# Up projection: the transfers that put aside the sums of pairs, begun by ScalarE in place of GpSimd

## The chip, the cores and the metric

The kernel runs on one core of one Trainium2 chip. The time is the device time of one execution in microseconds (us). A core has five engines that each work through their own list of instructions in order: TensorE (PE, with its weight loads, PEld), VectorE (DVE), ScalarE (ACT), GpSimd (POOL) and SyncE (SP). Transfers between the chip's DRAM and the on-chip SBUF are begun by an instruction on one of these lists (here on SP's, POOL's or ACT's) and are then carried by 16 DMA engines; an instruction that needs their data waits on a semaphore that the transfer raises when it has landed.

## The reference

One layer of a diffusion backbone: 512 latent tokens and 256 context tokens of width 2048, all in float32. A modulated RMS norm, one input projection, attention beside a gated short convolution, an output projection, then the gated MLP that this change concerns, and a final norm. The MLP, cut to what matters:

```
def dwconv3(x, w, b):
    xp = jnp.pad(x, ((0, 0), (1, 1), (0, 0)))
    return xp[:, :-2] * w[0] + xp[:, 1:-1] * w[1] + xp[:, 2:] * w[2] + b

def conv_ffn(h, w_up, cw, cb, w_down):          # FFN_DIM = 5504 = 43 tiles of 128
    u = dwconv3(h @ w_up, cw, cb)
    a, g = jnp.split(u, 2, axis=-1)
    return (a * jax.nn.silu(g)) @ w_down
```

## The kernel before

Activations lie transposed: features on the 128 partitions, the 512 tokens along a row, in two halves of 256 (H0, H1). Float32 operands are split in a high part that the TensorE takes as it is (a cast on ACT, line 1023 for weights) and a low part (the difference, on DVE, line 1024).

**Up projection.** A loop over `f` runs through 43 tiles of the hidden width; a step makes one tile of the gate (`cg`) and one of the value (`ca`). From `f` = 3 on, a step is a two-by-two block product in seven products instead of eight (weights `a11`, `a12`, `a22` and the sums `s1`, `s3`; operands of the tokens prepared once, the tiles `hf` and `T`). In the trace the products of step 12 are called u12p1, u12p2, u12p6, u12q5, u12p7, u12q4 and u12q3. p1, p6, p7 and q4 add up in one bank of PSUM, `u12a`; between them ACT must copy the partial sum out (`aside`, line 1224) before PE may go on adding to that bank. Steps overlap: q4 and q3 of a step run among p1, p2 and p6 of the next. The high and low parts of the weights live in three buffers each (`wh`, `wl`), so ACT can cast at most a product or so ahead of PE.

**Weights.** `up_load` (lines 1141 to 1152) has SP load five tiles of 512 KB per step; to two of them (`s1`, `s3`) a second block of weights is added by an accumulating transfer that POOL begins (line 1151, in the trace `u_s<-in_w_up`), as soon as the first has landed.

**Sums of pairs.** The down projection after it is a block product of the same kind, so it needs seven sums of each pair of activation tiles. `pair_sums` makes them while the up projection runs, for 18 pairs (steps 7 and 8, 9 and 10, and so on): `put` (lines 1065 to 1076) takes a source of 256 tokens, casts its high part into a tile `tp` on ACT (line 1074), has DVE write the low part behind it (line 1075), and begins a transfer of the tile, 256 KB, to the DRAM tensor `t_d` (line 1076). There are 126 of them, named in the program after the pair and the sum, `tp13` for sum "3" of pair 1. `pair_sums` is a generator that is advanced by one sum after every second product. The `tp` tiles come from pools with hardly a spare buffer at this time: the tile of sum "21" takes the place of the tile of sum "3" of the same pair, so its cast (line 1074) can't start before the transfer of sum "3" has landed.

**What sets the order.** The program is written in one order, and a scheduler with a simulated clock then decides how the instructions stand on each engine; only a few are tied (`tc.issue_after` puts the cast of a `put` behind the last cast of weights). An engine takes its list strictly in order. A transfer begun by SP or by ACT raises one of eight semaphores, which both use in turn; those begun by POOL have eight of their own. Where a semaphore is used again, its last transfer must have landed before the next is begun.

Of the kernel before, what the change touches and what calls it, by code (L numbers as in the profile page):

```python
# [10 lines left out]
F32 = mybir.dt.float32  # L11
# [61 lines left out]
def block_kernel(ctx, tc, xt, ctxt, ctxn, c, c_ctx, w_ada, small, w_in, w_inc, w_q, w_kv, w_out,  # L73
# [3 lines left out]
    V, A, G_, PE, SP = nc.vector, nc.scalar, nc.gpsimd, nc.tensor, nc.sync  # L77
# [15 lines left out]
    t_d = dr.tile([PAIRS, 7, P, T], F32, name="t_d")  # L93
# [3 lines left out]
    def t2(shape, dt, name):  # L97
        return act.tile(shape, dt, tag="t2", bufs=NT2, name=name)

    def tmp(shape, dt, name):  # L100
        return tp.tile(shape, dt, tag="tmp", bufs=5, name=name)
# [956 lines left out]
    OPS = ("11", "21", "2", "1", "3", "4", "22")  # L1058

    def pair_sums(p, e, o):  # L1060


        t = tmp([P, T], F32, f"ts{p}") if p == PAIRS - 1 else cp.tile([P, T], F32, tag="ts", bufs=1, name=f"ts{p}")

        def put(n, src):

            nth["tp"] += 1
            if nth["tp"] % 3 or p == PAIRS - 1:
                z = t2([P, T], F32R, f"tp{p}{n}")
            else:  # L1070
                z = cp.tile([P, T], F32R, tag="tq", bufs=1, name=f"tp{p}{n}")

            with tc.issue_after(last_hi[0]):
                A.copy(out=z[:, :256], in_=src)  # L1074
            V.tensor_tensor(out=z[:, 256:], in0=src, in1=z[:, :256].bitcast(F32), op=ALU.subtract)  # L1075
            G_.dma_start(t_d[p, OPS.index(n)], z.bitcast(F32))  # L1076

        put("11", e[:, H0])
        yield
        V.tensor_tensor(out=t[:, H0], in0=e[:, H0], in1=e[:, H1], op=ALU.subtract)  # L1080
        put("1", t[:, H0])
        yield
        V.tensor_tensor(out=e[:, H1], in0=o[:, H1], in1=e[:, H1], op=ALU.subtract)
        put("3", e[:, H1])
        yield
        put("22", o[:, H1])
        yield
        V.scalar_tensor_tensor(out=t[:, H1], in0=t[:, H0], scalar=-1.0, in1=o[:, H1], op0=ALU.mult, op1=ALU.subtract)
        put("2", t[:, H1])
        yield  # L1090
        put("21", o[:, H0])
        yield
        V.scalar_tensor_tensor(out=o[:, H0], in0=t[:, H1], scalar=-1.0, in1=o[:, H0], op0=ALU.mult, op1=ALU.subtract)
        put("4", o[:, H0])
        yield
# [378 lines left out]
    for st in range(STEPS - 2):  # L1474
        z = nxt
# [172 lines left out]
```

## Time and profile before

| | |
|---|---|
| median of 3 runs | 2161.89 us (2161.41, 2161.89, 2166.99) |
| profiled execution | 2159.29 us, of it 2157.2 us between its first and last instruction (the span) |
| PE busy in the span | 2095.5 us, 97% |
| DVE, ACT, POOL busy | 1825.5, 1046.5 and 187.9 us |
| mean granted TensorE clock | 0.991 of full speed |
| steps of the up projection by block products | from about 880 us to 1693 us |
| casts of `put` (line 1074), first and last | 1001.1 and 1739.8 us |

"Busy" counts the time in which an engine executes; beginning a transfer is not counted on SP and ACT. Where a row gives idle time and a releaser (`<-`), the engine stood that long before the instruction, and the releaser is what came last. An engine's idle time costs something only where PE then stands too. TensorE's clock is granted in stretches, and a row of a time window shows the mean clock in it (1.00 is full speed).

### The profile page before, as it was taken

The numbers are of one execution on the slowest core, as the hardware profiler recorded it, in microseconds if no ns is written. First come the engines' busy times: TensorE is split into PE (matmuls) and PEld (weight loads), VectorE is DVE, ScalarE is ACT, GpSimd is POOL, SyncE is SP. The second block draws the span as 40 slices with busy tenths as digits, with TensorE's granted clock in tenths as the row PEclk, the third lists the DMA queues.
The fourth block names the chain that finished last, engine by engine and source line by source line (L and its number), as shares of the span: only waits on it lengthen the run. The fifth ranks groups of instructions, "written<-read, shape, count | busy, mean of one in ns | idle before, by whom it ended". The sixth has DMA issues, their size and how long they took to land.

```text
span 2157.2 us, 35425 instructions
## 1 busy us (share of the span) xinstructions
PE 2095.5 (97%) x13268; PEld 1883.6 (87%) x13268; DVE 1825.5 (85%) x3024; ACT 1046.5 (49%) x1715; POOL 187.9 (9%) x270
## 2 busy tenths in 40 slices
PE   7899999999999999999999999999999999999997
PEld 4688788888888889999899898989989889999997
DVE  7998987778886989898889898888989748888887
ACT  5533333555553237555556555555555433333445
POOL 0000000000000000111111111211111100000000
PEclk9999999999999999999999999999999999999998
DMA  9989885334559985687778777778778999878683
GB/s 336 337 279 342 269 281 178 129 125 158 181 199 349 364 277 178 166 221 205 224 210 233 219 230 226 212 227 229 221 224 235 345 311 303 258 235 243 201 252 113
DMA packets 162112, 513.75 MB, mean 238 GB/s; under 512 B 18962, under 2 KB 23314, under 8 KB 156306
## 3 DMA queue, kind: packets, MB, share of 16 engines
q1 hardware_dynamic: 133364, 418.14, 56.7%
q0 software_dynamic: 27488, 92.29, 18.1%
q8 instruction: 104, 1.70, 0.3%
q10 hardware_dynamic: 1088, 1.05, 0.1%
q14 instruction: 68, 0.56, 0.1%
HBM read 464.22 MB, written 46.14 MB: 237 GB/s over the span
## 4 chain that ended last, share of the span: by engine, by line
PE 78%; DMA 11%; DVE 7%; issue 2%; ACT 2%; POOL 0%; DVEq 0%; SPq 0%; POOLq 0%; ACTq 0%
DMA t_d<-tp 4%; PE pp L187 4%; PE pp L189 4%; PE pp L188 3%; DMA u_s<-in_w_up 3%; DMA ada<-in_w_ada 2%; PE o L189 1%; PE o L187 1%; PE o L188 1%; PE d L187 1%; PE d L189 1%; PE d L188 1%; PE uf L187 1%; PE uf L188 1%; PE uf L189 1%
## 5 line engine op out<-in xcount | busy, mean ns | idle before, releaser
L1076 POOL DMA_DIRECT2D t_d<-tp x126 | 81.1, 657 | 442.5 <-DVE tp L1075 431.5
L1151 POOL DMA_DIRECT2D u_s<-in_w_up x80 | 70.1, 877 | 274.4 <-DMA u_s<-in_w_up 204.0
L263 DVE SCALAR_TENSOR_TENSOR ada<-ada,sv 128x1024 f32<-128x1024 f32 x68 | 82.3, 1223 | 12.4 <-DMA ada<-in_w_ada 12.4
L166 ACT CAST w_0h<-rw 128x512 fp32r<-128x512 f32 (+1 forms) x63 | 38.3, 618 | 105.9 <-PE pp L188 59.4
L241 DVE SCALAR_TENSOR_TENSOR ada<-ada,sv 128x1024 f32<-128x1024 f32 x64 | 78.2, 1230 | 5.8 <-DMA ada<-in_w_ada 5.6
L530 DVE SCALAR_TENSOR_TENSOR ada<-ada,svc 128x1024 f32<-128x1024 f32 x64 | 75.9, 1222 | 2.0 <-DMA ada<-in_w_ada 2.0
L1074 ACT CAST tp<-a 128x256 fp32r<-128x256 f32 x90 | 35.9, 406 | 67.6 <-DMA t_d<-tp 53.2
L793 POOL TENSOR_TENSOR gr<-gr,half 128x8 f32<-128x8 f32 x4 | 10.1, 2523 | 628.1 <-DVE gr L792 536.2
L167 DVE TENSOR_TENSOR w_0l<-rw,w_0h 128x512 fp32r<-128x512 f32 (+1 forms) x63 | 43.1, 691 | 22.1 <-ACT w_0h L166 21.8
L1075 DVE TENSOR_TENSOR tp<-a,tp 128x256 fp32r<-128x256 f32 x90 | 38.0, 423 | 24.6 <-ACT tp L1074 24.6
L263 DVE SCALAR_TENSOR_TENSOR ra<-ra,sv 128x1024 f32<-128x1024 f32 x44 | 52.5, 1220 | 1.1 <-DMA ra<-in_w_ada 1.0
L1265 DVE TENSOR_TENSOR u<-u,u_s 128x1024 f32<-128x1024 f32 x40 | 48.9, 1221 | 5.2 <-DMA u_s<-in_w_up 5.0
L1266 DVE TENSOR_TENSOR u<-u,u 128x1024 f32<-128x1024 f32 x40 | 48.8, 1220 | 0.0
L764 ACT CAST pth<-t 128x384 fp32r<-128x384 f32 x64 | 28.6, 485 | 26.7 <-PE t L761 26.7
L541 DVE TENSOR_TENSOR acc<-acc,pp 128x512 f32<-128x512 f32 x50 | 34.7, 693 | 2.1 <-PE pp L189 2.1
L765 DVE TENSOR_TENSOR ptl<-t,pth 128x384 fp32r<-128x384 f32 x64 | 33.3, 552 | 2.7 <-ACT pth L764 2.7
L745 DVE TENSOR_REDUCE mn<-s 128x1 f32<-128x768 f32 x32 | 30.4, 954 | 5.1 <-PE s L734 4.9
L1038 ACT ACTIVATE g<-g 128x512 f32<-128x512 f32 x43 | 27.2, 632 | 15.2 <-DVE g L1032 14.8
L1030 ACT ACTIVATE g<-cg,sm 128x512 f32<-128x512 f32 x40 | 32.6, 815 | 0.0
L1030 ACT ACTIVATE a<-ca,sm 128x512 f32<-128x512 f32 x40 | 32.1, 802 | 0.0
L748 ACT ACTIVATE p<-s,mn 128x768 f32<-128x768 f32 x32 | 29.3, 915 | 1.6 <-DVE mn L745 1.3
L1032 DVE SCALAR_TENSOR_TENSOR a<-ca,sm,a 128x511 f32<-128x511 f32 x40 | 29.9, 747 | 0.0
(10239 smaller groups left out, 8970.6 us busy)
## 6 DMA issues: line engine op xcount, KB each, us to landing
ada<-in_w_ada SPq DMA_DIRECT2D x196, 512.0 KB, 5.9
u<-in_w_up SPq DMA_DIRECT2D x120, 512.0 KB, 8.9
w<-t_d SPq DMA_DIRECT2D x161, 256.0 KB, 5.0
u_s<-in_w_up SPq DMA_DIRECT2D x80, 512.0 KB, 4.0
u_s<-in_w_up POOLq DMA_DIRECT2D x80, 512.0 KB, 9.7
t_d<-tp POOLq DMA_DIRECT2D x126, 256.0 KB, 8.6
v<-in_w_dnw SPq DMA_DIRECT2D x72, 384.0 KB, 5.1
ra<-in_w_ada SPq DMA_DIRECT2D x22, 1024.0 KB, 4.7
```

Source lines behind the costliest of these rows:

```text
L167: V.tensor_tensor(out=lo[:, :n], in0=raw[:, a:a + n], in1=hi[:, :n].bitcast(F32), op=ALU.subtract)
L187: PE.matmul(ps, w[0], x[0], start=first, stop=False, skip_group_check=on_top)
L188: PE.matmul(ps, w[0], x[1], start=False, stop=False, skip_group_check=on_top)
L189: PE.matmul(ps, w[1], x[0], start=False, stop=last, skip_group_check=on_top)
L241: V.scalar_tensor_tensor(out=r, in0=r, scalar=1.0, in1=vec[:, i * 1024:(i + 1) * 1024], op0=ALU.mult, op1=ALU.mult, accum_out=col[:, i:i + 1])
L263: keep(V.scalar_tensor_tensor(out=r, in0=r, scalar=1.0, in1=svs[i], op0=ALU.mult, op1=ALU.mult, accum_out=lc[:, t % 4:t % 4 + 1] if i else ...
L530: keep(V.scalar_tensor_tensor(out=raw[q], in0=raw[q], scalar=1.0, in1=svc[:, q * 1024:(q + 1) * 1024], op0=ALU.mult, op1=ALU.mult, accum_o ...
L1030: A.activation(u, src, AF.Identity, bias=s("fb", m), scale=s("fw", 86 + m))
L1076: G_.dma_start(t_d[p, OPS.index(n)], z.bitcast(F32))
L1151: G_.dma_start(r[-1], src[more], accum_op=ALU.add)
L1265: V.tensor_tensor(out=a11, in0=a11, in1=s1, op=ALU.add)
L1266: V.tensor_tensor(out=a12, in0=a12, in1=a11, op=ALU.add)
```

## The change

One word: the transfer at the end of `put` is begun on ACT's list instead of POOL's. Each of the 126 transfers waits, as before, for DVE's part of the tile (line 1075).

```
             with tc.issue_after(last_hi[0]):
                 A.copy(out=z[:, :256], in_=src)
             V.tensor_tensor(out=z[:, 256:], in0=src, in1=z[:, :256].bitcast(F32), op=ALU.subtract)
-            G_.dma_start(t_d[p, OPS.index(n)], z.bitcast(F32))
+            A.dma_start(t_d[p, OPS.index(n)], z.bitcast(F32))
```

The scheduler then moves instructions on other engines too, each by a few places. Three places matter below. A minus marks a row that stood there before, a plus a row that stands there now; the number behind a name counts tiles through the program.

POOL's list around steps 10 to 12 (`u_s` are the weights `s1` and `s3`):

```order
 L1151 DMA u_s_9774<-in_w_up 128x1024
 L1151 DMA u_s_9777<-in_w_up 128x1024
-L1076 DMA t_d<-tp_9923 128x512
-L1076 DMA t_d<-tp_9978 128x512
-L1076 DMA t_d<-tp_10104 128x512
 L1151 DMA u_s_9991<-in_w_up 128x1024
-L1076 DMA t_d<-tp_10054 128x512
 L1151 DMA u_s_9994<-in_w_up 128x1024
```

Only the accumulating transfers stay on POOL's list in this part of the program.

ACT's list in step 12, where `tp_10501` is sum "3" and `tp_10551` sum "22" of pair 1:

```order
 L1074 CAST tp_10551<-a_10336 128x256
 L1023 CAST u12p6h<-u_11_10208 128x1024
+L1076 DMA t_d<-tp_10501 128x512
+L1076 DMA t_d<-tp_10551 128x512
+L1230 ACTIVATE ca_10431<-u11a 128x256
 L1023 CAST u12q5h<-u_s_10212 128x1024
 L1074 CAST tp_10618<-ts_10369 128x256
-L1230 ACTIVATE ca_10431<-u11a 128x256
```

The two transfers stand behind the cast for product p6 and ahead of that for q5. In other pairs (step 14, for example) sum "22" comes first and sum "3" second at the same place.

ACT's list in step 14, where `tp_11146` is sum "21" of pair 2 and `u_11042` the copy of bank `u14a` that product p7 waits for:

```order
 L1023 CAST u15p1h<-u_11_10881 128x1024
+L1074 CAST tp_11146<-a_10783 128x256
 L1224 COPY u_11042<-u14a 128x256
-L1074 CAST tp_11146<-a_10783 128x256
 L1038 ACTIVATE g_11004<-g_11004 128x512
 L1023 CAST u15p2h<-u_12_10883 128x1024
+L1076 DMA t_d<-tp_11146 128x512
 L1023 CAST u14q4h<-u_22_10665 128x1024
```

The cast of sum "21" now stands ahead of the copy. Before, it stood ahead of it in six steps (10, 12, 18, 24, 30 and 36) and behind it in ten (14, 16, 20, 22, 26, 28, 32, 34, 38 and 40); now it stands ahead of it in all sixteen.

On PE's list the first matrix product of q4 (or of p2, or of q3) is placed a few rows earlier in some steps, and on SP's list a few loads after the up projection change places.

More of the change, by code (lines that the diff above doesn't have):

```diff
@@ L1075, in put @@
             V.tensor_tensor(out=z[:, 256:], in0=src, in1=z[:, :256].bitcast(F32), op=ALU.subtract)
-            G_.dma_start(t_d[p, OPS.index(n)], z.bitcast(F32))
+            A.dma_start(t_d[p, OPS.index(n)], z.bitcast(F32))
         put("11", e[:, H0])
```

## The prediction

> **What bounds the kernel now.** I read the groups of instructions first, because the change touches three of them: the transfers of `put`, the accumulating transfers beside them, and the casts that start each `put`.
>
> ```profile
> L1076 POOL DMA_DIRECT2D t_d<-tp x126 | 81.1, 657 | 442.5 <-DVE tp L1075 431.5
> L1151 POOL DMA_DIRECT2D u_s<-in_w_up x80 | 70.1, 877 | 274.4 <-DMA u_s<-in_w_up 204.0
> L1074 ACT CAST tp<-a 128x256 fp32r<-128x256 f32 x90 | 35.9, 406 | 67.6 <-DMA t_d<-tp 53.2
> ```
>
> POOL stands 204.0 us for weights to land before it may accumulate; POOL's own idle time costs nothing, but a transfer of `put` that is ready stands behind it. The third row shows the consequence: ACT stands 53.2 us for a transfer of `put` to land. Whether that matters is told by PE's waits alone, from 1000 us to the end of the `put`s:
>
> ```profile
> PE u36a L187 <- ACT u L1224: 2.5, 1, 2.5
> PE u18a L187 <- ACT u L1224: 2.3, 1, 2.3
> PE u24a L187 <- ACT u L1224: 2.3, 1, 2.3
> PE u30a L187 <- ACT u L1224: 2.1, 1, 2.1
> PE u10a L187 <- ACT u L1224: 2.0, 1, 2.0
> PE u12a L187 <- ACT u L1224: 2.0, 1, 2.0
> PE d L187 <- ACT dw00h L1023: 1.0, 1, 1.0
> ```
>
> In six steps PE waits for the copy of line 1224 ahead of product p7, 13.2 us together. The chain of waits says what made the copy late in step 12:
>
> ```profile
> 1065.24 0.50 POOL u_s L1151
> 1065.74 0.06 issue
> 1065.80 10.15 DMA t_d<-tp
> ...
> 1075.97 0.03 ACT tp L1074
> ...
> 1076.29 0.38 ACT u L1224
> ...
> 1076.70 0.38 PE u12a L187
> ```
>
> POOL accumulates (it had waited for the load), then begins the transfer of sum "3"; this takes 10.15 us; ACT's cast of sum "21" waits for it, the copy stands behind the cast, PE behind the copy. A step's whole price is read from windows of one step each (from the first matrix product of p2 to the next step's). The columns are length, PE busy (matrix products), clock, DMA share, GB/s:
>
> ```profile
> 1040.49:1060.24 19.75, 19.75 (x138) 1.00 0.82 226
> 1016.99:1040.49 23.50, 21.50 (x139) 0.93 0.70 202
> 1552.18:1576.24 24.06, 21.55 (x139) 0.93 0.69 200
> 1368.80:1389.19 20.39, 20.24 (x139) 1.00 0.75 211
> 1408.96:1429.67 20.71, 20.28 (x138) 1.00 0.77 225
> 1077.73:1081.15 3.41, 3.41 (x18) 0.50 0.71 238
> 1693.21:1697.21 4.00, 4.00 (x19) 1.00 1.02 400
> ```
>
> An undisturbed step is PE without a gap, 19.75 to 19.78 us. The second and third rows are the first and last of the six disturbed steps (the others 23.53, 23.86, 23.84 and 23.67): 142.46 together against 6 x 19.77 = 118.62, so 23.84 us lost. Of this 13.2 is the waiting; the other 10.6 is the clock, which after each of these waits is granted at half speed for 3.41 us (sixth row: 18 matrix products where 29 would fit). After the wait of only 1.0 us at `dw00h` it stays at 1.00 (last row). Two more steps, 20.39 and 20.71, are 0.62 and 0.94 long: there ACT's longest waits made the weights late.
>
> **The change, part by part.** *Removed:* 126 beginnings on POOL, on no path themselves, and with them the queue behind the accumulations. *Added on ACT:* the same 126. Their price on a list, and the time to landing in nearby rows (256 KB each):
>
> ```profile
> L1464 ACTq DMA_DIRECT2D out<-out x4: 378/378/417, 2149.0 to 2152.6; - x4
> out<-out ACTq DMA_DIRECT2D x4, 256.0 KB, 2.9
> w<-t_d SPq DMA_DIRECT2D x161, 256.0 KB, 5.0
> t_d<-tp POOLq DMA_DIRECT2D x126, 256.0 KB, 8.6
> DMA to landing us min/median/max: 3.3/8.6/13.0
> ```
>
> At 0.38 to 0.42 us, 126 cost ACT 53 us at most, which would all count if ACT had no room; it is busy 1046.5 us of 2157.2. The dangerous part is that a transfer waits on ACT's list for DVE, and a cast of weights is queued behind it. Laying the new order over the rows of before, ACT arrives ahead of DVE's half in 32 of 126 places, by at most 1.4 us. A typical one, sum "2" ahead of the cast for p7 of step 14:
>
> ```profile
> 1111.49 0.42 DVE L1075 TENSOR_TENSOR tp<-ts,tp 128x256 fp32r<-128x256 f32 x1
> 1112.26 1.05 ACT L1023 CAST u14p7h<-u_s 128x1024 fp32r<-128x1024 f32 x1 [1.36 <-PE u13c L196]
> 1117.82 0.29 PE L187 MATMUL u14a<-hf0h,u14p7h 128*128 128x256 f32 x1
> ```
>
> ACT gets there about 1 us early. DVE is done at 1111.91, the transfer is begun by about 1112.4, and the cast moves from 1112.26 to 1112.5. PE wants it at 1117.82, 4.5 us after it was ready. That cover is why I cost the 126 at nothing; without it each such place would cost about 1 us.
>
> *Moved:* the moment a transfer starts. In step 12, sum "3":
>
> ```profile
> 1063.17 0.42 DVE L1075 TENSOR_TENSOR tp<-a,tp 128x256 fp32r<-128x256 f32 x1
> 1063.19 1.05 ACT L1023 CAST u12p6h<-u 128x1024 fp32r<-128x1024 f32 x1 [0.94 <-PE u12b L196]
> 1074.43 0.28 PE L188 MATMUL u13a<-hf0l,u13p1h 128*128 128x256 f32 x1
> 1106.46 1.05 ACT L1023 CAST u14p6h<-u 128x1024 fp32r<-128x1024 f32 x1 [0.91 <-PE u14b L196]
> ```
>
> ACT ends the cast for p6 at 1064.24 and can begin the transfer at once, 1.5 us before POOL did. PE is out of other work at 1074.71 and starts 0.73 us after the cast of sum "21" (1075.97 to 1076.70). So PE doesn't wait if the transfer lands by 1073.98, in 9.7 us. Where sum "3" is begun second, as in step 14, ACT begins it at about 1107.51 + 0.42 = 1107.93; PE wants p7 at 1117.82, so it must land by 1117.09, in 9.2 us.
>
> This limit now counts in all sixteen pairs, since the cast stands ahead of the copy in all of them. Before, in ten, ACT's wait lay behind the copy and cost PE nothing. So the landing time decides the sign. Its bounds are 2.9 us (last stage, hardly any other traffic) and 13.0 (the slowest on POOL's queue). I take about 6.5: nearer to SP's 256 KB at 5.0 in a busy stage than to POOL's 8.6, because in step 12 POOL's transfer had 512 KB of accumulation, begun 0.56 us earlier, ahead of it in one queue, and ACT's has none. At 6.5, even at 9, PE doesn't wait.
>
> [...] The traces of before do not show ACT's queue in a busy stage.
>
> *The end of the up projection.* SP's loads and ACT's transfers now share eight semaphores in turn. Within the loop the earlier user has landed 5 us or more before the next wants it, by the issue times of before and 8.6 us to landing. After step 42 it is tight, since SP's loads then come in bursts. First hit would be the second weights of the down projection:
>
> ```profile
> 1700.13 1.23 DVE L1024 TENSOR_TENSOR dw01l<-d,dw01h 128x1024 fp32r<-128x1024 f32 x1 [4.71 <-ACT dw01h L1023]
> 1703.11 0.40 PE L187 MATMUL d<-yl1h,dw01h 128*128 128x512 f32 x1
> ```
>
> They are ready 1.75 us early. ACT has a transfer ahead of that cast that may wait for a load of SP, which may wait for an earlier transfer of ACT: 0 to 3.5 us late by the landing times above, so 0 to 4 us for PE with the clock. I take 1.
>
> **Sum**, against the profiled execution: 2159.3 - 23.8 (six steps) - 1.6 (two steps) + 1 (end) + 1 (scattered leftover, 0 to 6) = 2135.9. The median of the runs lies 2.6 above the profiled execution, so 2138.5; I say 2138. What would be late next is the accumulated `s1`, which DVE needs soon after it lands, but its bytes and competitors are the same.
>
> **Rivals.**
>
> 1. *The transfer is as slow as before where it matters*, 10.15 us, because all queues share the engines. For it speaks the DMA share of 0.82 in an undisturbed step. It lands 0.5 us after the limit in step 12's kind and 1.0 in step 14's: 16 x 0.8 = 13 us of short waits, and a wait of 1.0 left the clock alone. 2138 + 13 = 2151.
> 2. *The other side: sixteen pairs stall instead of six.* One mechanism, the place of the cast ahead of the copy: if sum "3" lands 11.5 us or more after it is begun, PE waits about 2 us and the clock halves, as in the six steps, 3.97 each. That is 16 x 3.97 - 23.8 = 40 us more: 2200. It is slower than before from 1.6 us per pair (25.4 / 16), a landing of about 11 us. For it speaks the maximum of 13.0; against it, that those long ones stood behind accumulations.
> 3. *ACT's list takes the gain back*: each transfer that waits for DVE holds casts for p1 or p6, which have less cover than p7. If each of the 18 pairs lost 1.4 us this way, 25 us, the time would be 2162. Against it, ACT stands ahead of most casts for PE to free a buffer anyway (1.36 in the row of step 14).
>
> **Chances.** Forecast 0.69, first rival 0.14, second 0.10, third 0.07. A run of this kernel tells about 0.3%, 6.5 us, from no change. The forecast and most of the first rival (0.10 of it) are faster by more, 0.79; the rest of it and the third are the same, 0.11; the second is slower, 0.10. The range goes from 2131 (the whole 25.4 and some of the end) to 2158, which takes in the first rival and leaves out most of the others. The forecast's own range is 2131 to 2146.
>
> **What would show it.** Right: in the profile after, ACT's casts of line 1074 no longer wait for `t_d<-tp`, or under 1 us each; PE's waits for line 1224 ahead of p7 are gone; the mean clock rises in the loop; steps 10 to 42 all take 19.8 us; transfers of ACT land in 5 to 9 us. Wrong: PE waits for line 1224 in ten other steps (second rival), or waits of PE for line 1023 or 1024 in the loop (third), or a landing above 9.7 us (first). A pause of PE at the weights `dw01` would put the loss at the end.

## The result and the profile after

The changed kernel takes 2138.72 us in the median of 4 runs (2131.61 to 2140.45), the kernel before, run beside it, 2161.65 (2156.61 to 2166.99): a ratio of 0.9887, 95% interval 0.9854 to 0.9921, 23 us faster. The profiled executions are 2159.29 us before and 2137.18 after.

Three rows of the page of the profile after: the accumulating transfers, the casts of `put`, and the moved transfers with their time to landing. Then all that PE waits for from 1000 us to the end of the `put`s.

```profile
L1151 POOL DMA_DIRECT2D u_s<-in_w_up x80 | 68.5, 856 | 684.1 <-DMA u_s<-in_w_up 364.4
...
L1074 ACT CAST tp<-a 128x256 fp32r<-128x256 f32 x90 | 35.7, 403 | 4.8 <-DMA yl6h<-y_d 3.5
...
t_d<-tp ACTq DMA_DIRECT2D x126, 256.0 KB, 6.0
```

```profile
PE d L187 <- ACT dw00h L1023: 1.0, 1, 1.0
```

POOL still stands for weights, longer than before, and nothing is behind it now. ACT's 53.2 us of waiting for `t_d<-tp` are gone (the 3.5 us that are left are another transfer's, after the loop), and so are PE's six waits for the copy of line 1224. The moved transfers take 6.0 us to land in the median, 8.6 before. (The trace has a landing for 95 of the 126 after the change, and for all before; medians of landings here and below go by those that it has.)

Windows of the loop, before and then after, from the first matrix product of p2 of step 9 to the first of the down projection, and one step after. Columns: length, PE busy, PEld, DVE, ACT, POOL, clock, DMA share, GB/s.

```profile
997.21:1693.21 696.00, 681.20 (x4603) 631.29 (x4601) 613.50 (x898) 390.47 (x594) 122.81 (x184) 0.99 0.78 225
```

```profile
999.37:1019.15 19.78, 19.78 (x139) 18.39 (x137) 17.19 (x24) 11.11 (x16) 1.69 (x2) 1.00 0.78 212
...
999.37:1670.07 670.70, 669.68 (x4603) 622.39 (x4601) 612.08 (x898) 391.91 (x594) 56.23 (x66) 1.00 0.82 233
```

The loop is 25.3 us shorter: PE's idle time falls from 14.80 to 1.02 us, and its busy time by 11.52 us with the same 4603 matrix products. Of this, 10.2 us is the half-speed clock that no longer occurs (half of six times 3.41 us), and about 1 us the two longer steps. All steps take 19.8 us (in five places two steps have to be taken together, since the first matrix product of p2, from which a step is counted, is placed earlier there: 39.61 us for steps 12 and 13). Ahead of this stretch the profiled execution after is 2.2 us longer, and behind it 1.3 us (span less start: 465.3 against 464.0), in parts that the change hardly touches; so the spans differ by 21.8 us, and the profiled times by 22.1.

Why sum "3" lands early is seen in step 12 (timeline of ACT's and POOL's lists, put together; then the landing of the first of the two transfers):

```profile
1062.06 0.99 ACTq L1076 DMA_DIRECT2D t_d<-tp  x2
...
1063.74 0.86 POOL L1151 DMA_DIRECT2D u_s<-in_w_up  x1 [16.27 <-DMA u_s<-in_w_up]
```

```profile
DMA to landing us min/median/max: 5.8/5.8/5.8
```

ACT begins sum "3" 1.7 us ahead of POOL's accumulation; before, POOL began it 0.56 us behind. It lands in 5.8 us where 10.15 were needed. The runs below ask which of the two did it, the own queue or the earlier moment.

### The profile page after: what moved, and what is told of

Its sections match the earlier page's. It is cut to its first block, busy times and chain, and to the rows that moved or that the text cites. A ratio compares the mean times of both kernels' runs of the same rounds, so it can differ in the third digit from the quotient of the medians.

```text
span 2135.4 us, 35321 instructions
## 1 busy us (share of the span) xinstructions
PE 2084.9 (98%) x13268; PEld 1875.9 (88%) x13268; DVE 1824.1 (85%) x3024; ACT 1047.1 (49%) x1715; POOL 117.0 (5%) x144
## 4 chain that ended last, share of the span: by engine, by line
PE 89%; DVE 5%; DMA 4%; ACT 2%; issue 1%; SPq 0%; DVEq 0%; POOLq 0%; ACTq 0%
PE pp L187 4%; PE pp L189 4%; PE pp L188 4%; PE o L189 1%; PE o L188 1%; PE o L187 1%; PE d L187 1%; PE d L189 1%; PE d L188 1%; DMA ada<-in_w_ada 1%; PE uf L187 1%; PE uf L188 1%; PE uf L189 1%; PE of L187 1%; PE of L188 1%
## 5 line engine op out<-in xcount | busy, mean ns | idle before, releaser
L793 POOL TENSOR_TENSOR gr<-gr,half 128x8 f32<-128x8 f32 x4 | 10.1, 2522 | 631.3 <-DVE gr L792 538.9
L1031 DVE SCALAR_TENSOR_TENSOR g<-cg,sm,g 128x511 f32<-128x511 f32 x40 | 29.8, 745 | 0.0
```

The costliest lines, as they stand in the source:

```text
L1031: V.scalar_tensor_tensor(out=u[:, 1:], in0=src[:, :T - 1], scalar=s("fw", m), in1=u[:, 1:], op0=ALU.mult, op1=ALU.add)
```

## The experiments

All were timed beside the kernel before. "Against s1" is when sum "3" was begun, against the first accumulation of the same step (a plus is later), in step 12; the landing is the median over the sixteen pairs of steps 10 to 40, each transfer matched with its place in the list (of sum "3" begun by ACT or SP the trace has 11 to 13 of the 16 landings, and 5 in experiment 4; of sum "3" begun by POOL it has all); the last column counts steps in which PE waited for the copy ahead of p7.

| | kernel | median us | ratio, 95% | sum "3" begun by, against s1 | landing us | PE stalls at p7 |
|---|---|---|---|---|---|---|
| | before | 2161.65 | | POOL, +0.56 | 10.1 | 6 |
| | the change | 2138.72 | 0.9887 (0.9854, 0.9921) | ACT, -1.68 | 5.8 | 0 |
| 1 | only sum "3" by ACT | 2137.78 | 0.9883 (0.9847, 0.9918) | ACT, -1.70 | 5.7 | 0 |
| 2 | all but sum "3" by ACT | 2181.77 | 1.0088 (1.0060, 1.0116) | POOL, +0.54 | 10.6 | 11 |
| 3 | before, copy first | 2142.22 | 0.9911 (0.9878, 0.9944) | POOL | 10.0 | 0 |
| 4 | 252 halves by ACT | 2139.40 | 0.9888 (0.9862, 0.9914) | ACT | 5.2 (second half) | 0 |
| 5 | two more transfers ahead | 2197.54 | 1.0152 (1.0120, 1.0184) | ACT | 11.7 | 2 |
| 6 | the same, copy first | 2195.73 | 1.0157 (1.0130, 1.0185) | ACT | 11.3 | 0 |
| 7 | by SP | 2137.30 | 0.9881 (0.9852, 0.9910) | SP, -1.80 | 5.7 | 1 (0.2 us) |
| 8 | before, no adding | 2149.72 | 0.9939 (0.9921, 0.9957) | POOL, +0.53 | 9.0 | 6 |
| 9 | before, s1 behind sum "3" | 2137.40 | 0.9871 (0.9849, 0.9893) | POOL, -1.43 | 5.4 | 0 |
| 10 | the change, sum "3" later | 2164.53 | 0.9989 (0.9970, 1.0008) | ACT, +0.84 | 9.7 | 11 |
| 11 | 10 without accumulations | 2140.39 | 0.9900 (0.9863, 0.9937) | ACT, none | 5.5 | 0 |

### Which of the 126 transfers matter: experiments 1 and 2

```
-            A.dma_start(t_d[p, OPS.index(n)], z.bitcast(F32))
+            (A if n == "3" else G_).dma_start(t_d[p, OPS.index(n)], z.bitcast(F32))
```

> Only the 18 transfers of sum "3" are begun by ACT, the other 108 stay on POOL's list. Theory (the gain is the landing of sum "3" alone: ACT's cast of sum "21" waits for it, the copy of line 1224 stands behind that cast, and PE's p7 behind the copy): nearly the whole gain of the change with a seventh of its transfers, 2137 to 2144 us; no wait of PE for line 1224 ahead of p7, sum "3" lands in 5 to 9 us, no half-speed window in the loop. Rival (POOL's queue must be emptied, since all 126 transfers slow the accumulations and the weights): a seventh of the gain, about 3 us, 2158.

Experiment 2 has `G_` and `A` the other way round.

> The mirror image: 108 transfers are begun by ACT, only those of sum "3" stay on POOL's list, behind the accumulations. ACT's list has the cast of sum "21" ahead of the copy in all sixteen pairs, as in the change. Theory (landing of sum "3" alone): the gain is lost. Those that begin behind an accumulation take about 10 us as in step 12 of the kernel before; six to sixteen pairs lose 3.97 us each on top of 2138, so 2162 to 2201. Rival (POOL's queue relieved of most transfers): six sevenths of the gain, about 2142. Rival (the order of the lists, not the queue, brings the gain): 2138.

Experiment 1, sum "3" on ACT's list (18 transfers, 12 of them with a landing in the trace; least, median, most):

```profile
DMA to landing us min/median/max: 5.1/5.7/6.1
```

Experiment 2, sum "3" on POOL's list, who waited for it, and the longest and shortest of PE's waits at p7:

```profile
  ACT tp L1074: 45.3, 11
...
DMA to landing us min/median/max: 4.9/10.5/12.1
```

```profile
PE u38a L187 <- ACT u L1224: 3.9, 1, 3.9
...
PE u20a L187 <- ACT u L1224: 2.2, 1, 2.2
```

Eighteen of the 126 transfers carry the whole gain; without them the other 108 make the kernel slower than before, since the cast of sum "21" now stands ahead of the copy everywhere. This is the other side that the second rival described. Its price is read from the window of the loop:

```profile
1000.26:1718.07 717.81, 686.18 (x4603) 636.84 (x4601) 616.00 (x898) 390.54 (x594) 65.64 (x83) 0.98 0.77 218
```

These are 47.1 us more than the 670.70 after the change, 4.3 for each of the eleven stalls. Only eleven and not sixteen pairs stall: in steps 12, 18, 24, 30 and 36 the cast of sum "21" starts 3.3 to 4.3 us before sum "3" has landed (in step 12 at 1074.35, the landing at 1077.77). There it waits for the semaphore of sum "22" and not of sum "3", so it uses another tile. After the change it is not so: the cast of sum "21" waits for the semaphore of sum "3" in all sixteen.

### Is it the cast ahead of the copy: experiment 3

```
+    copies = []
-            with tc.issue_after(last_hi[0]):
+            with tc.issue_after(copies[-2] if n == "21" and p < PAIRS - 1 else last_hi[0]):
-        A.copy(out=r, in_=ps[:, :256])
+        copies.append(A.copy(out=r, in_=ps[:, :256]).ins)
```

(against the kernel before, transfers on POOL's list)

> The kernel before, every transfer on POOL's list, with one thing changed: the cast of sum "21" is tied behind the copy that p7 waits for, so that it stands behind it in all sixteen pairs instead of ten. Theory (the slow landing costs only through the cast that stands ahead of the copy): the landings stay at 8.6 us in the median, ACT still waits for them some 50 us, but PE's six waits for line 1224 and their half-speed windows are gone; about 23 us less than before, 2138 to 2145 (a pair of steps with late weights may keep 0.6 to 0.9 us each). Rival (the slow transfers themselves slow the loop, by weights or by bandwidth): most of the loss stays, 2150 to 2162.

ACT's waits for the transfers, and PE's in the neighbourhood of the longest of them (step 15):

```profile
ACT tp L1075 <- DMA t_d<-tp: 70.2, 16, 5.6
```

```profile
PE u15b L197 <- DVE u15p2l L1025: 0.8, 1, 0.8
...
PE u15b L196 <- ACT u15p2h L1024: 0.3, 1, 0.3
```

The landings stay at 10 us and ACT waits longer than before (70.2 us against 53.2), yet all six stalls and half-speed windows are gone (the mean clock of the profiled execution is 0.995, as after the change; 0.991 before). So the slow landing costs through the cast ahead of the copy. What is left is of the kind of the steps of 20.39 and 20.71 in the kernel before: ACT's wait makes the weights of the next p2 late, and a step up to 1.5 us longer where ACT waited over 5 us. In the profiled execution the loop is 684.55 us, 13.9 longer than after the change; that execution took 2151.35 us, the other three 2141 to 2142.

### ACT's list and a late landing: experiments 4, 5 and 6

```
-            A.dma_start(t_d[p, OPS.index(n)], z.bitcast(F32))
+            for i in range(2):
+                A.dma_start(t_d[p, OPS.index(n)][:, HS[i]], z[:, HS[i]].bitcast(F32))
```

> The change with each of the 126 transfers cut into two halves of 128 KB, so that ACT begins 252. Theory (ACT's beginnings are hidden): 126 more beginnings of 0.35 us, 44 us more on ACT's list, cost PE nothing; 2135 to 2145. Rival (ACT's list is paid by PE): if the 126 beginnings of the change already cost a part of the gain, 126 more cost as much again; the full 44 us would give 2183, the 25 us of the third rival of the prediction 2163.

```profile
t_d<-tp ACTq DMA_DIRECT2D x252, 128.0 KB, 7.2
```

126 more beginnings cost nothing that can be measured (0.9888 against 0.9887), so ACT's list has the room. This doesn't double the waits for DVE, since the first half needs ACT's part of the tile alone. What decides on the third rival is PE's list of waits after the change: in the loop PE waits for no cast.

Experiment 5 puts two transfers ahead of that of sum "3", and experiment 6 adds to it the tie of experiment 3.

```
+            for i in range(2 if n == "3" else 0):
+                A.dma_start(t_x[p, i], z.bitcast(F32))
             A.dma_start(t_d[p, OPS.index(n)], z.bitcast(F32))
```

> The change, with two further transfers of the same tile (256 KB each, to a DRAM tensor that nothing reads) begun by ACT just ahead of the transfer of sum "3", so that this one lands later. It prices the second rival of the prediction. In the trace after the change the landing may take 9.8 to 10.2 us before PE waits at p7, and it takes 5.8. Theory (landing and limit alone decide): with 512 KB more ahead of it in ACT's queue the landing takes 10 to 14 us; from about 10 us on each pair loses what lies above the limit and, from about 2 us of waiting on, the half-speed window, 3.5 to 5 us in all, in up to sixteen pairs: 2150 to 2215. If the landing stays under 9.8 us: no wait of PE and 2139. Rival (moving the beginnings is what helped, a late landing costs nothing): 2139 whatever the landing.

> The kernel of the run above (two further transfers ahead of that of sum "3"), and the cast of sum "21" tied behind the copy that p7 waits for. Theory (a late landing costs through the cast ahead of the copy): the landing stays as late as in the run above, ACT waits for it behind the copy, and PE doesn't: 2139 to 2148, the upper end if late weights cost some 0.5 us in each pair as in the run with POOL's transfers and the copy first (2142). Rival (the added bytes slow the loop by themselves): as slow as the run above.

Both came out at 2196 to 2198. Experiment 5 doesn't test what it was made for, though its time lies in the expected range: the scheduler saw the longer transfers and put the cast of sum "21" behind the copy in ten pairs, as in the kernel before. PE waits there for the weights of p2, and for the copy ahead of q4 in nine steps (ten in experiment 6). Experiment 6 is a miss: copy first didn't save it. ACT's list in step 14 of experiment 6:

```profile
1120.22 0.37 ACT L1228 COPY u<-u14a 128x256 f32<-128x256 f32 x1
1125.03 0.41 ACT L1076 CAST tp<-a 128x256 fp32r<-128x256 f32 x1 [4.44 <-DMA t_d<-tp]
1125.34 0.81 ACT L1032 ACTIVATE g<-cg,sm 128x512 f32<-128x512 f32 x1
...
1126.76 1.03 ACT L1025 CAST u15p2h<-u 128x1024 fp32r<-128x1024 f32 x1
```

```profile
PE u15b L198 <- DVE u15p2l L1026: 1.1, 1, 1.1
PE u14a L197 <- ACT u L1228: 1.0, 1, 1.0
```

The copy for p7 was in time; but the same wait of 4.4 us, with two activations now behind it, makes the weights of the next p2 and then the next copy late, about 1 us each, and the step that begins there (15) takes 24.04 us, at a mean clock of 0.93. So here a late landing costs behind the copy too, and "copy first" is a cure only while the list behind the waiting cast has slack. How much of the loss comes this way isn't told apart: the added bytes slowed their neighbours as well (the accumulations of the loop land in 10.6 and 10.3 us in experiments 5 and 6, in 9.7 after the change), as the rival of experiment 6 had it. The two don't price the second rival; experiment 2 does, for eleven pairs.

### Queue or moment: experiments 7 to 11

Experiment 7 has `SP.dma_start` at that place. Experiment 8 is the kernel before with `G_.dma_start(r[-1], src[more])` in line 1151, without `accum_op`; it leaves out the addition, so s1 and s3 hold their second block of weights alone.

> The 126 transfers begun by SP, whose list also holds the loads of weights. ACT's list has the cast of sum "21" ahead of the copy in all sixteen pairs. Theory (a queue without accumulations is enough): the transfers land in 5 to 9 us, the nearest rows of SP's queue being 5.2 us for 256 KB in the last stage and 9.0 us for a load of 512 KB; under the limit of about 10 us, so 2136 to 2145, if SP's waits for DVE don't make loads late (SP stands idle ahead of loads for some 600 us already, so there is room). Rival (a transfer queued behind loads of 512 KB is as late as behind accumulations): landings of 10 us or more, eleven to sixteen pairs lose about 4 us each, 2180 to 2205.

> The kernel before, with the same instructions in the same order on every engine, but POOL's 80 transfers of the second block of weights don't add: they overwrite the first block (the sums s1 and s3 are left out). It tells whether the accumulation or the queue is what delays sum "3" on POOL's list. Theory (accumulation is what is slow: 9.7 us for 512 KB against 4.3 us for SP's load of the same tile): sum "3" lands in 5 to 7 us instead of 10.1, no wait of PE at p7, 2136 to 2145 as with the change. Rival (any 512 KB ahead in the same queue delay it as much): landings stay at 9 to 10 us, six stalls stay, 2155 to 2165.

Experiment 7, the transfers on SP's list; experiment 8, the transfers that overwrite, and the longest and shortest wait of PE at p7:

```profile
t_d<-tp SPq DMA_DIRECT2D x126, 256.0 KB, 5.9
```

```profile
u_s<-in_w_up POOLq DMA_DIRECT2D x80, 512.0 KB, 8.3
```

```profile
PE u24a L187 <- ACT u L1224: 2.1, 1, 2.1
...
PE u10a L187 <- ACT u L1224: 0.5, 1, 0.5
```

With SP the gain is the same, although its queue holds loads of 512 KB. So it needn't be ACT. In experiment 8, with each list as before, taking the adding away shortens the landing of sum "3" by 1.1 us only, to 9.0: neither 5 to 7 as the theory said nor unchanged. Six shorter stalls stay (6.9 us together). The adding is the smaller part.

This left two readings: a queue without 512 KB ahead, or the moment. In the kernel before, sum "22" stands ahead of the accumulation in eleven pairs and lands in 5.25 us in the median of all sixteen, on POOL's own list; after the change, sums "11", "1" and "2" land in 9.6, 7.8 and 8.8 us on ACT's. Experiments 9 and 10 set the one against the other. Experiment 9 is the kernel before with the first accumulation of a step tied behind sum "3":

```
+            with tc.issue_after(begun.pop()) if begun else ExitStack():
+                G_.dma_start(*owed.pop(0), accum_op=ALU.add)
...
-            G_.dma_start(t_d[p, OPS.index(n)], z.bitcast(F32))
+            i = G_.dma_start(t_d[p, OPS.index(n)], z.bitcast(F32)).ins
+            if n == "3":
+                begun[:] = [i]
...
         product(pb, a12, "21", f"u{f}p2", True)
+        pay()
```

(`up_load` notes the accumulations in `owed`, and `pay` begins them.)

> The kernel before, every transfer on POOL's list and in POOL's queue, with one thing changed: the first accumulating transfer of a step (weights s1) is written behind the transfer of sum "3", so that POOL begins sum "3" ahead of it in all sixteen pairs, without standing for the weights first. ACT's list has the cast of sum "21" ahead of the copy in all sixteen pairs, as in the change. Theory A (the place ahead of the accumulation decides, whatever queue carries the transfer): sum "3" lands in 5 to 6 us, as sum "22" does in the kernel before where it stands ahead (5.25 us in the median, sum "3" behind it 10.1); no wait of PE at p7; 2136 to 2143, the whole gain without ACT. Theory B (the prediction's second reason: a queue of its own, without accumulations, makes the transfer faster): it still shares POOL's queue and lands in 8 us or more, limit about 8 to 10 us; 2155 to 2200.

Experiment 10 is the change with sum "3" kept until ACT has cast the weights for q5 (`put` notes its transfer in `kept`):

```
         product(pc, s1, "1", f"u{f}q5", True)
+        while kept:
+            with tc.issue_after(last_hi[0]):
+                A.dma_start(*kept.pop())
```

> The counterpart: the change, with the transfer of sum "3" tied behind ACT's cast for product q5, so that ACT begins it some 2 to 4 us later, behind POOL's accumulation in time, though still in ACT's own queue. The cast of sum "21" stands ahead of the copy in all sixteen pairs. Theory A (the moment ahead of the accumulation decides): it lands in 8 to 10 us, as ACT's transfers of sums "11", "1" and "2" do in the change (9.6, 7.8 and 8.8 us in the median), where about 6 are left before PE waits; eleven to sixteen pairs lose about 4 us each, 2180 to 2210. Theory B (the queue of its own decides): it lands in 5 to 6.3 us as before the delay, PE waits under 0.5 us a pair, 2138 to 2146.

POOL's list in step 12 of experiment 9, with the landing of its first row:

```profile
1065.66 0.54 POOL L1076 DMA_DIRECT2D t_d<-tp  x1 [11.17 <-DVE tp L1075]
1067.09 0.89 POOL L1150 DMA_DIRECT2D u_s<-in_w_up  x1 [0.89 <-DMA u_s<-in_w_up]
```

```profile
DMA to landing us min/median/max: 5.0/5.0/5.0
```

Experiment 10, step 12 of POOL's and ACT's lists, then the 17 late transfers of line 1280 (who waited for them; landings, of which the trace has 13):

```profile
1070.32 0.86 POOL L1155 DMA_DIRECT2D u_s<-in_w_up  x1 [16.15 <-DMA u_s<-in_w_up]
...
1071.16 0.33 ACTq L1280 DMA_DIRECT2D t_d<-tp  x1
```

```profile
  ACT tp L1075: 34.8, 11
...
DMA to landing us min/median/max: 4.9/9.6/11.7
```

Theory A is met twice. On POOL's list, ahead of the accumulation, sum "3" lands in 5.4 us and the kernel takes 2137.40, the whole gain with no transfer moved to ACT. On ACT's list and in ACT's queue, 0.84 us behind the accumulation, it lands in 9.7 us, eleven pairs stall, and the gain is gone (2164.53; the expected 2180 to 2210 is missed because a stall costs less here, see the last section). The window of its loop:

```profile
1001.83:1697.14 695.31, 674.16 (x4602) 624.58 (x4601) 615.42 (x898) 390.64 (x594) 56.33 (x66) 1.00 0.80 225
```

These are 24.6 us more than after the change, 2.2 for each of the eleven stalls.

How far ahead of an accumulation is enough was not tried. After the change sum "2" begins about 0.9 us ahead of the second accumulation of its step, with the first still in flight, and lands in 8.8 us.

Experiment 11 is experiment 10 without line 1151 at all; it leaves out the second block of weights, so s1 and s3 hold their first block alone, and 42 MB are not moved.

> The run before (sum "3" begun by ACT some 2.4 us later than in the change), with the 80 accumulating transfers of the loop left out, so that the weights s1 and s3 are their first block alone and 42 MB less are moved. SP's loads stay. It tells what makes the late transfer slow. Theory (the accumulation that begins within a microsecond of it): sum "3" lands in 5 to 6.5 us instead of 9.7, no wait of PE at p7, 2137 to 2145. Rival (SP's load of 512 KB, which begins in the same microsecond, or the load of s3 ahead of it): it still lands in 8 us or more and PE still waits in eleven pairs, 2155 to 2165.

```profile
DMA to landing us min/median/max: 5.2/5.5/5.9
```

SP's loads, in experiment 10 and then in 11:

```profile
u<-in_w_up SPq DMA_DIRECT2D x120, 512.0 KB, 9.4
```

```profile
u<-in_w_up SPq DMA_DIRECT2D x120, 512.0 KB, 5.5
```

Begun at the same late place, sum "3" lands in 5.5 us. SP's loads, which begin in the same microsecond, are still there, and are themselves faster. So it is POOL's transfers of line 1151 that slow what begins with them, in ACT's queue and in SP's alike.

## Why the prediction was right, and where not

- **What bounds the kernel; six steps and two.** Right. 23.8 + 1.6 = 25.4 us were to go from the loop; 25.3 went, with all the marks named: no wait of ACT for `t_d<-tp`, no wait of PE for line 1224, no half-speed window, steps of 19.8 us. Experiment 3 shows that the path (landing, cast, copy, p7) is the cause: it was broken at the cast alone, and the stalls went.
- **126 beginnings at nothing.** Right; twice as many cost nothing either. One took 0.33 us, not 0.38 to 0.42.
- **Landing about 6.5 us, under the limit of 9.2 to 9.7.** Nearly: 5.8 (5.2 to 6.3), and by the start of PE's p7 after the change 9.8 to 10.2 were allowed. ACT did not have to end its cast for p6 first, as the prediction had it: in step 12 the cast starts at 1061.61 and takes 1.05 us, and the transfer is begun at 1062.06.
- **Why it would land early.** The reason given for the 6.5 failed in part: "in step 12 POOL's transfer had 512 KB of accumulation, begun 0.56 us earlier, ahead of it in one queue, and ACT's has none". The queue made no difference: experiment 9 gets 5.4 us in POOL's queue, experiment 10 gets 9.7 in ACT's. What decides is the moment, which the prediction had in passing and did not use for the landing: ACT "can begin the transfer at once", and so ahead of the accumulation, because on ACT's list no instruction that stands for weights is in front of it. That a number taken from rows of other places, for a reason that half failed, came within 1 us is in part luck.
- **Which engine begins it.** That did not alter how fast sum "3" landed: 5.4 us begun by POOL (experiment 9) and 5.8 by ACT ahead of the accumulation, 10.1 by POOL and 9.7 by ACT (experiment 10) behind it. The 10.15 us of the first rival belonged to a moment, and the moment moved: on ACT's list the transfer no longer stood behind an instruction that waits.
- **"This limit now counts in all sixteen pairs."** Right for the changed kernel: in all sixteen the cast stands ahead of the copy and waits for the semaphore of sum "3" (in step 12 that transfer landed at 1067.88, and the cast started at 1070.98). Experiments 2 and 10 stall in eleven, because their five other pairs use another tile.
- **The price of the second rival.** A stall was put at 3.97 us; it was 4.3 in experiment 2 and 2.2 in experiment 10. With the eleven pairs of experiment 2, at 4.3, the rival's sum is 2138 + 47 = 2185, and experiment 2 measured 2182. A late landing in all sixteen, the rival's 2200, was not run.
- **The first rival** (10.15 us stays) and **the third** (ACT's list) are refuted: the first by the landing of 5.8 us, the third by the absence of any wait of PE for a cast in the loop, and by experiment 4.
- **End and leftover, 1 us each.** Neither is seen. PE's only wait there is the 1.0 us at `dw00h` that was there before. ACT stood 3.5 us for the transfer `yl6h`, just ahead of its cast for `dw10h`, and 4.5 us at the weights `dw11h`; before the change it stood 3.6 and 4.6 us at these two casts already, so no price of the shared semaphores shows. In place of the 2 us the profiled execution lost 3.5 us ahead of and behind the stretch (2.2 + 1.3), and came to 2137.18 where the sum said 2135.9. The median then lay 1.5 us above the profiled execution, not 2.6 as before the change. That the forecast of 2138 is met within 1 us is so in part luck: the two differences cancel.

## What to carry to other kernels

A short transfer placed on the list of an engine that stands for data is late by that wait, and then competes with what the engine begins (sum "3", begun 0.56 us behind the accumulation, took 10.15 us to land); move it ahead on the same list (5.4 us in experiment 9) or to a list that isn't waiting (5.8 after the change), and look at when it begins against the big transfers, not at whose queue it is in. When a landing time is carried over from one place of a program to another, ask what was in flight there (sum "3" took 9.7 us with POOL's accumulations and 5.5 without them, in experiments 10 and 11). A cast that waits for a buffer should stand behind what TensorE needs next (a ratio of 0.9911 in experiment 3), but that only passes the lateness to the next thing on the list (a step of 24.04 us in experiment 6).

## What the runs showed of the hardware that was not expected

A stall of about 2 us did not always halve the clock. In the kernel before, the clock was 0.50 for 3.41 us after each of the six stalls, whose waits were 2.0 to 2.5 us; in the 3.41 us just ahead of these stretches PE was idle for 1.90 to 2.51 us. Two waits of experiment 10, in steps 10 and 26 (2.4 and 2.3 us), in windows of 3.41 us:

```profile
1035.15:1038.56 3.41, 0.99 (x7) 0.70 (x6) 1.70 (x4) 0.80 (x3) 0.00 (x0) 1.00 1.06 283
1038.56:1041.97 3.41, 3.41 (x16) 3.41 (x17) 3.22 (x5) 1.36 (x2) 0.00 (x0) 0.50 0.74 253
1362.83:1366.24 3.41, 1.79 (x12) 1.41 (x10) 2.20 (x3) 0.03 (x1) 0.00 (x0) 1.00 1.03 287
1366.24:1369.65 3.41, 2.71 (x22) 2.72 (x23) 2.83 (x4) 2.11 (x4) 0.00 (x0) 1.00 0.97 317
1369.65:1373.06 3.41, 3.41 (x29) 3.32 (x28) 2.87 (x5) 1.74 (x3) 0.00 (x0) 1.00 0.08 31
```

In the first row PE is idle for 2.42 us, and the clock of the second row is 0.50. The second wait lies in two rows, with 1.62 and 0.70 us of idle time, and the clock is 1.00 in both and in the row after them. Step 10 took 23.97 us, at a mean clock of 0.93; steps 14, 26 and 40, whose waits were 2.0, 2.3 and 2.2 us, took 22.03, 22.41 and 22.25 us, at 1.00. So a stall cost 3.97 us in the kernel before, where half speed followed each of the six, and 2.2 in the mean of the eleven of experiment 10. What decides whether half speed follows such a wait was not shown.

With POOL's 512 KB accumulations in the loop (experiment 10), sum "3" of 256 KB and SP's loads of 512 KB alike took 4 us longer than without them (experiment 11): 9.7 against 5.5 us, and 9.4 against 5.5. How much of this is the 512 KB and how much the way in which POOL's transfers are carried stays open: experiment 8 shows only that the adding is 1.1 us of it. Why five of the sixteen pairs use another tile in experiments 2 and 10 than after the change stays open too.
